# A two-layer hybrid block: the DeltaNet's chunk transitions formed ahead of the scan, attention's value products for two heads on the column halves, modulation products in pairs

## The chip, the cores and the metric

The kernel runs on one core of a Trainium2 chip. Its time is the device time of that core in microseconds (us), from runs of the same program. Everything is float32; the large products split each float32 operand into two float32r parts and take three float32r products, the small ones use float32 directly.

## What is computed

The reference runs two layers over 512 latent tokens and 256 context tokens with 1024 channels. Each layer modulates its normalised input by a shift and a scale computed from a conditioning vector, projects it once, and hands the columns to three mixers: a gated MLP over chunks of 128 tokens, attention (six query heads, two key heads of 64 channels), and a gated DeltaNet in both directions (six heads of 64). An output projection, a squared-ReLU MLP and post-norms follow. In the second layer only the latent tokens give outputs. For the change these parts matter:

```python
def _attend(q, k, v):
    s = jnp.einsum('bqhgd,bkhd->bhgqk', q, k).astype(jnp.float32) * (HEAD_DIM ** -0.5)
    pr = jax.nn.softmax(s, axis=-1).astype(v.dtype)
    return jnp.einsum('bhgqk,bkhd->bqhgd', pr, v)
...
    # gated_delta_rule, chunks of 64 tokens; u, w solve the chunk's triangular system
    def step(s, inp):
        qd, kd, u_i, w_i, a_i, gl = inp
        v_new = u_i - jnp.einsum('bhck,bhkv->bhcv', w_i, s)
        o = jnp.einsum('bhck,bhkv->bhcv', qd, s) + jnp.einsum('bhij,bhjv->bhiv', a_i, v_new)
        s = s * jnp.exp(gl)[..., None, None] + jnp.einsum('bhck,bhcv->bhkv', kd, v_new)
        return s, o
...
        mod_l = (jax.nn.silu(c) @ mod_w[i] + mod_b[i])[:, None, :]
```

## The kernel before

`Flow` interleaves streams of work, Python generators that yield after each step. Each engine runs its instructions in the order in which they were traced; `Flow.cost` guesses a duration for every instruction, and the stream whose last step ends first by that guess goes on next. Streams also wait for named signals (`conv…`, `prep…`, `made…`, `scan…`, `po…`) and for PSUM tiles, of which there are four of 512 columns ("mm") and two of 1024 ("ax").

`mix` runs one layer's mixers in three stages: input modulation with the gated MLP's projections; convolutions, query and key norms (`qk_norm`), values and the gate of z (`z_gate`), with the DeltaNet's preparation (`dn_prep`) of head pairs 0 and 1 beside them; then attention beside the scans, with `dn_prep` of pair 2. In layer 0 the last stage also holds `mods`, two pieces of the modulation (`mod`). `rest` follows with the output projection and the MLP.

In the last stage there are three scan streams, one for each pair of heads, and three streams that form their operands. The streams of the DeltaNet have a head start of 1000 ns (`BIAS`) over attention. Pairs 0 and 1 run side by side; pair 2 uses the buffers of pair 0 and its preparation must end first. A scan has six step pairs; a step pair has two steps, and each step takes one chunk forward and one backward, on the two halves of the partitions.

For each step pair `dn_make` scales keys, values and queries (gs, rU, rK), transposes some, and copies all into block-diagonal 128x128 operands in a ring of buffers (rW, rT, rK, rQ, rA), whose zero quarters GpSimd fills at the start of the stage; the triangular inverse comes in by small DMAs (rT). `dn_scan` then needs in each step, one after the other: a product with W, a subtraction (rr), a product with T, a copy (vn), a product with K and the state's update (S); where outputs are wanted, four more products and two instructions that write or add them to o. Each product runs for both heads of the pair, ten in a step. `dn_gate` norms and gates the outputs of a pair.

`attention` takes a tile of 128 queries and a head at a time: scores, maximum (amx, anm), exponential with its sum (ape), reciprocal (ars). `att_out` transposes the exponentials, copies them (apT), multiplies them by the values of both key heads (128 columns, of which 64 are used), scales the result (aot), and after six heads transposes the outputs (ayb). `mod` multiplies a conditioning vector, 32 columns wide, by 512 columns of weights at a time into one of four groups of 32 partitions of a PSUM tile.

Of the kernel before, what the change touches and what calls it, by code (L numbers as in the profile page):

```python
# [39 lines left out]
class Flow:  # L40
    """Interleaves streams of work (generators that yield after each step) as they are traced. The engines run what is
    traced in order, so the stream whose last step ends first, by a rough cost of each instruction, goes on next. A stream
    yields a generator to start it, a key to wait until that key is in `done`, a tuple of classes of PSUM tiles to get,
    or the time to go on."""

    # wait for a result of the same engine, of another one
# [68 lines left out]
    def when(self, s):  # L115
        """the time a stream can go on, None while what it waits for is not there"""
# [11 lines left out]
    def run(self, *gens, side=(), drain=False):  # L128
        """until the streams gens end; those of side go on in the next run if they have not ended, or else with drain"""
# [37 lines left out]
    def step(self, gen, val, ahead):  # L167
        """one step of a stream, its instructions as if they were traced that much earlier"""
# [19 lines left out]
    def drop(self, ap):  # L188
        """gives a PSUM tile back, after the last instruction on it"""
# [21 lines left out]
class _Core:  # L211
    """the engines, with a note of all that is issued to them"""
# [6 lines left out]
def _tb(v):  # L219
    """token tile whose chunks the backward direction takes at step pair v (the forward one takes tile v)"""  # L220
# [63 lines left out]
class K:  # L284
# [22 lines left out]
    def setup(self):  # L307
# [21 lines left out]
        nc.vector.memset(self.mhalf, -0.5)  # L329
# [1607 lines left out]
```

## Time and profile before

| | |
|---|---|
| median of 3 runs | 2101.53 us (2100.57 to 2102.2) |
| span of the profiled execution | 2099.3 us |
| TensorE busy | 1944.5 us, 93% |
| VectorE, ScalarE, GpSimd busy | 1358.6, 921.4, 195.3 us |
| stage of attention and scans, layer 0 | 304 to 576 us |
| the same, layer 1 | 1463 to 1668 us |

PE is TensorE's matmuls, PEld its weight loads, DVE is VectorE, ACT ScalarE, POOL GpSimd, SP the engine that issues the loads. The profile gives the span of one execution from its first to its last instruction; the runs' time is some 2 us longer. Busy time is the union of an engine's instructions. A float32 matmul appears as two records. Matmuls overlap in the array, so that the end of a record is not where the next may start. PEclk is the granted clock, 1.00 for 2.4 GHz and 0.50 for 1.2 GHz. What stands behind `<-` in brackets is what an idle engine waited for.

### The profile page before, as it was taken

The page shows a single profiled execution, that of the slowest core. Times are in us where ns is not written, and L with a number is a line of the kernel's source. Part 1 is how long each engine was busy: PE and PEld are TensorE (multiplying, and loading weights), DVE is VectorE, ACT ScalarE, POOL GpSimd, SP SyncE. Part 2 cuts the span into 40 slices and gives each one's busy share as a digit, 9 for nine tenths or more (in the row PEclk, how much of TensorE's full clock was granted, in tenths as well). Part 3 has the DMA queues.
Part 4 walks back from the last instruction along what each step waited for, and adds up shares of the span by engine and source line. Part 5 has one row for each costly group of instructions (what it writes and reads, how often), then busy time and mean ns, then how long its engine had stood idle before and what let it go on. Part 6 is the DMA issues. An engine that isn't in the chain of part 4 may idle for free. (4 is left out here: it accounts for less than half of the span.)

```text
span 2099.3 us, 31005 instructions
## 1 busy us (share of the span) xinstructions
PE 1944.5 (93%) x11870; PEld 1601.5 (76%) x11870; DVE 1358.6 (65%) x2659; ACT 921.4 (44%) x1881; POOL 195.3 (9%) x375
## 2 busy tenths in 40 slices
PE   6999779989898999999999989997988889999998
PEld 2887655678777888888888778875877768788886
DVE  5578887865577436362457777889896485544555
ACT  4444346566645322322232265443866445422341
POOL 1111221010012000000000111122100010000001
PEclk8999989989999999999999979977999999999999
DMA  7311024312335424241445243110101434322231
GB/s 280 103 46 51 16 75 149 117 40 64 112 110 181 132 72 159 81 140 43 139 161 173 98 142 95 53 36 26 34 23 30 166 129 164 107 90 81 96 107 59
DMA packets 98240, 208.91 MB, mean 100 GB/s; under 512 B 30850, under 2 KB 45058, under 8 KB 98092
## 3 DMA queue, kind: packets, MB, share of 16 engines
q1 hardware_dynamic: 86956, 189.24, 27.9%
q10 hardware_dynamic: 11136, 17.70, 2.2%
q8 instruction: 93, 1.52, 0.3%
q14 instruction: 55, 0.45, 0.1%
HBM read 184.38 MB, written 17.79 MB: 96 GB/s over the span
## 5 line engine op out<-in xcount | busy, mean ns | idle before, releaser
L206 ACT ACTIVATE whi<-wraw 128x1024 fp32r<-128x1024 f32 (+2 forms) x188 | 194.9, 1050 | 440.6 <-PE ax L206 287.8
L206 DVE TENSOR_TENSOR wlo<-wraw,whi 128x1024 fp32r<-128x1024 f32 (+2 forms) x188 | 226.4, 1211 | 224.6 <-ACT whi L206 224.1
L206 PE MATMUL mm<-x2xh,whi 128*128 128x256 f32 (+1 forms) x832 | 288.4, 347 | 10.5 <-ACT whi L206 9.0
L206 PE MATMUL mm<-x2xh,wlo 128*128 128x256 f32 (+1 forms) x832 | 287.3, 346 | 1.6 <-DVE wlo L206 1.6
L206 PE MATMUL mm<-x2xl,whi 128*128 128x256 f32 (+1 forms) x832 | 287.7, 346 | 0.0
L206 PE MATMUL ax<-whi,hh 128*128 128x512 f32 x640 | 251.2, 392 | 0.0
L206 PE MATMUL ax<-whi,hl 128*128 128x512 f32 x640 | 250.0, 391 | 0.0
L206 PE MATMUL ax<-wlo,hh 128*128 128x512 f32 x640 | 249.9, 390 | 0.0
L206 PEld LDWEIGHTS mm<-x2xh,whi 128*128 128x128 f32 x832 | 158.9, 191 | 34.1 <-ACT whi L206 9.4
L206 DVE TENSOR_TENSOR acc<-acc,ax 128x1024 f32<-128x1024 f32 x68 | 82.9, 1219 | 148.3 <-PE ax L206 148.1
L206 PEld LDWEIGHTS mm<-x2xh,wlo 128*128 128x128 f32 x832 | 158.6, 191 | 22.6 <-DVE wlo L206 2.4
L206 PEld LDWEIGHTS mm<-x2xl,whi 128*128 128x128 f32 x832 | 158.8, 191 | 19.9
L206 PEld LDWEIGHTS ax<-whi,hh 128*128 128x128 f32 x640 | 120.2, 188 | 29.7 <-ACT hh L206 5.2
L206 PEld LDWEIGHTS ax<-whi,hl 128*128 128x128 f32 x640 | 120.1, 188 | 27.5 <-DVE hl L206 2.9
L206 PEld LDWEIGHTS ax<-wlo,hh 128*128 128x128 f32 x640 | 120.2, 188 | 27.0 <-issue 2.6
L206 ACT ACTIVATE rl<-mm 128x256 f32<-128x256 f32 (+1 forms) x104 | 50.7, 490 | 129.1 <-PE mm L206 123.7
L206 DVE SCALAR_TENSOR_TENSOR acc<-modw,cz,acc 128x1024 f32<-128x1024 f32 x80 | 101.2, 1280 | 8.4 <-DMA acc<-in_mod_b 5.4
L206 POOL TENSOR_SCALAR rs<-mv 128x1 f32<-128x1 f32 x52 | 33.1, 637 | 699.1 <-DVE mv L206 696.8
L206 PE MATMUL mm<-ava,apT 128*128 128x128 f32 x624 | 88.4, 285 | 2.7 <-ACT apT L206 1.2
L206 PEld LDWEIGHTS mm<-ava,apT 128*128 128x128 f32 x624 | 78.8, 197 | 7.2 <-ACT apT L206 3.2
L206 DVE TENSOR_TENSOR hl<-rl,hh 128x768 fp32r<-128x768 f32 (+2 forms) x76 | 54.4, 716 | 29.4 <-ACT hh L206 29.4
L206 DVE SCALAR_TENSOR_TENSOR cacc<-cb,cw,cacc 128x772 f32<-128x772 f32 (+1 forms) x72 | 69.7, 972 | 0.7 <-ACT cacc L206 0.2
(255 smaller groups left out, 4178.5 us busy)
## 6 DMA issues: line engine op xcount, KB each, us to landing
wraw<-in_w_up SPq DMA_DIRECT2D x64, 512.0 KB
wraw<-in_w_down SPq DMA_DIRECT2D x64, 512.0 KB
modw<-in_mod_w SPq DMA_DIRECT2D x56, 512.0 KB
modw<-in_mod_w SPq DMA_DIRECT2D x80, 256.0 KB
wraw<-in_w_ch SPq DMA_DIRECT2D x22, 512.0 KB
wraw<-in_w_out SPq DMA_DIRECT2D x16, 512.0 KB
x_d<-xt ACTq DMA_DIRECT2D x16, 512.0 KB
xt<-x_d SPq DMA_DIRECT2D x14, 512.0 KB
```

The costliest lines, as they stand in the source:

```text
L206: return f(*args, **kw)
```

## The change

DeltaNet: for each step pair `dn_make` now forms, in 64x64 blocks of the two partition halves, w and u (wu), the transition of the state over a whole chunk P (the decay on the diagonal, less keys times w), its offset C, and the output's transition Q. `dn_scan` then takes P times the state plus C for each step; outputs are Q times the state plus A times u, summed over both directions once a step pair. The block-diagonal buffers, their fills, and the copies by DMA are gone. Scalings of keys and queries, the decay's diagonal and the outputs' sums move to GpSimd. A (products of queries and keys) is stored by direction, and the decays E by token. Operands of pair 2 wait for the last ones of pair 0.

Attention: 1/8 is folded into the queries, the maximum is negated as it is taken, the exponentials are divided by their sum before they are transposed, and the value products of two heads go to the two halves of the output's partitions, channels first, so that no transposition of outputs is left.

Modulation: weights come in pieces of 1024 columns, and two products on neighbouring groups are issued together. `z_gate` waits for the gate before it, the first one for all query and key norms. `Flow.cost` has new guesses for products of 64 or 32 columns of weights. In the diff below `dn_make` and `dn_scan` are shown as they are after the change, without the lines that they replace, which stand above.

```diff
+            if m == 64 and ins[0].shape[0] == 64:
+                return 0.9 * n
             if ins[-1].dtype == F32R:
                 return max(35.0 + 0.56 * m, 0.42 * n)
-            return 2.0 * max(35.0 + 0.62 * m, 0.83 * n)
+            if m == 32 and n == 512:
+                return n
+            return (1.0 if m == 64 else 2.0) * max(35.0 + 0.62 * m, 0.83 * n)
...
+        todo = [(k, g) for k in range(KD) for g in range(0, n, 2)]
...
+            nc.sync.dma_start(out=w, in_=d["mod_w"][l, j, k][:, 512 * g : 512 * g + 1024])
...
+        for i, (k, g) in enumerate(todo):
+            w = ws.pop(0)
             yield flow.ready[w.tensor.name][0]
-            nc.tensor.matmul(pm[32 * g : 32 * g + 32], self.cz[:, k, :], w, start=(k == 0), stop=(k == KD - 1))
-            if i + bufs < n * KD:
+            for b in range(2):
+                r = 32 * (g + b)
+                nc.tensor.matmul(
+                    pm[r : r + 32], self.cz[:, k, :], w[:, 512 * b : 512 * b + 512], start=(k == 0), stop=(k == KD - 1)
+                )
...
+            if p == 2:
+                yield f"made{l}05"
...
+        yield f"z{l}{t - 1}" if t > self.tiles[0] else f"qk{l}{LT[-1]}"
...
-                mx = self.small([P, 1], "amx")
-                nc.vector.tensor_reduce(out=mx, in_=ps, axis=AX.X, op=ALU.max)
                 nm = self.small([P, 1], "anm")
-                nc.vector.tensor_scalar(out=nm, in0=mx, scalar1=-0.125, scalar2=None, op0=ALU.mult)
+                nc.vector.tensor_reduce(out=nm, in_=ps, axis=AX.X, op=ALU.max, negate=True)
...
-                nc.vector.reciprocal(st["rs"][:, h : h + 1], su)
+                yield
+                rs = self.small([P, 1], "ars")
+                nc.vector.reciprocal(rs, su)
+                nc.vector.tensor_scalar(out=pe[:, 0:n], in0=pe[:, 0:n], scalar1=rs[:, 0:1], scalar2=None, op0=ALU.mult)
...
-        pT = ap_.tile([P, TOK], F32, tag="apT", bufs=1, name="apT")
+        pT = ap_.tile([P, TOK], F32, tag="apT", bufs=4, name="apT")
+        if h % 2 == 0:
+            st["pT"] = pT
...
-        po = yield from self.psum(P)
+        if h % 2 == 0:
+            self.flow.signal(f"po{l}{i}")
+            return
+        pv = yield from self.psum(P)
         for c in range(kts):
-            nc.tensor.matmul(po, pT[:, c * P : c * P + P], va[:, c].rearrange("p a b -> p (a b)"), start=(c == 0), stop=(c == kts - 1))
-        yield
-        nc.vector.tensor_scalar(out=st["ot"][:, h, :], in0=po[:, HD * (h // 3) : HD * (h // 3) + HD], scalar1=st["rs"][:, h : h + 1], scalar2=None, op0=ALU.mult)
-        self.drop(po)
+            for e, p in enumerate((st["pT"], pT)):
+                nc.tensor.matmul(
+                    pv[_half(e)], va[:, c, (h - 1 + e) // 3, :], p[:, c * P : c * P + P], start=(c == 0), stop=(c == kts - 1)
+                )
         self.flow.signal(f"po{l}{i}")
         yield
-        if h < NH - 1:
-            return
-        ot = st["ot"].rearrange("p h e -> p (h e)")
-        pt = yield from self.psum(384)
-        for a in range(3):
-            self.tr(pt[:, a * P : a * P + P], ot[:, a * P : a * P + P])
-        yield
-        y = ap_.tile([P, 3, P], F32, tag="ayb", bufs=1, name="ayb")
-        nc.scalar.copy(y, pt.rearrange("p (a b) -> p a b", a=3))
-        self.drop(pt)
-        yield from self.store(self.y_d[l, t, :, 2:5, :], y)
+        nc.scalar.copy(st["y"][:, h // 2, :], pv)
+        self.drop(pv)
+        yield
+        if h == NH - 1:
+            yield from self.store(self.y_d[l, t, :, 2:5, :], st["y"])
...
     def dn_make(self, l, p, v, qkv, G, A, TT, r):
         nc, sc = self.nc, self.dn
+        need = l == 0 or v > 1
+        kds, ks, egc, be, E = G["kds"], G["ks"], G["egc"], G["be"], G["E"]
         hs = slice(2 * p, 2 * p + 2)
+        td = (v, _tb(v))
+        a0 = 0 if l == 0 else 2
         he = lambda a: a.rearrange("p t (h e) -> p t h e", e=HD)
         q, k, vv = (he(qkv[:, w]) for w in range(3))
+        mul = lambda eng, o, a, s: eng.tensor_tensor(out=o, in0=a, in1=_col(s, HD), op=ALU.mult)
+        halves = [_half(f) for f in range(2)]
+        blk = [(d, h) for d in range(2) for h in range(2)]
+        mm = nc.tensor.matmul
+        T4 = TT.rearrange("p (d h t) c -> p d h t c", d=2, h=2)
+        new = lambda n, *sh: sc.tile([P, *sh], F32, tag=f"{n}{p % 2}", bufs=1, name=n)
+        kv, kd = new("kv", 2, 2, 2, HD), new("kd", 2, 2, HD)
+        for d, t in enumerate(td):
+            mul(nc.vector, kv[:, d, :, 0, :], k[:, t], ks[:, d, t, hs])
+        nc.scalar.copy(kv[:, 0, :, 1, :], vv[:, v])
+        mul(nc.vector, kv[:, 1, :, 1, :], vv[:, td[1]], be[:, 1, td[1], hs])
+        for d, t in enumerate(td):
+            mul(nc.gpsimd, kd[:, d], k[:, t], kds[:, d, t, hs])
+        yield
+        if need:
+            qd = new("qd", 2, 2, HD)
+            for d, t in enumerate(td):
+                mul(nc.gpsimd, qd[:, d], q[:, t], egc[:, d, t, hs])
+            yield
+        ei = new("ei", 2, 2, HD)
+        for d, t in enumerate(td):
+            nc.gpsimd.tensor_tensor(
+                out=ei[:, d], in0=self.id2.unsqueeze(1).broadcast_to([P, 2, HD]), in1=_col(E[:, d, t, hs], HD), op=ALU.mult
+            )
+        yield
+        ps = yield from self.psum(512)
+        for d, h in blk:
+            for f in halves:
+                o = P * (2 * d + h)
+                mm(ps[f, o : o + P], T4[f, d, h, td[d]], kv[f, d, h].rearrange("p a b -> p (a b)"), start=True, stop=True)
+        yield
+        wu = r["wu"]
+        nc.scalar.copy(wu.rearrange("p d h c -> p (d h c)"), ps)
+        self.drop(ps)
+        yield
+        ps, pc = yield from self.psum(512, 256)
+        for d, h in blk:
+            for i, f in enumerate(halves):
+                mm(ps[f, 256 * d + 64 * h : 256 * d + 64 * h + HD], wu[f, d, h, 0:HD], kd[f, d, h], start=True, stop=True)
+                e = i if d == 0 else 1 - i
+                o = P * e + 64 * h
+                mm(pc[halves[1 - i], o : o + HD], kd[f, d, h], wu[f, d, h, HD:P], start=True, stop=True)
+        for d, h in blk if need else ():
+            o = 256 * d + P + 64 * h
+            for f in halves:
+                mm(ps[f, o : o + HD], qd[f, d, h], self.id2[f], start=True, stop=False)
+            for f in halves:
+                mm(ps[f, o : o + HD], wu[f, d, h, 0:HD], A[f, d, h, td[d] - a0], start=False, stop=True)
+        yield
+        pv = ps.rearrange("p (d w c) -> p d w c", d=2, w=2)
+        nc.vector.tensor_tensor(out=r["P"], in0=pv[:, :, 0, :], in1=ei.rearrange("p d h c -> p d (h c)"), op=ALU.add)
+        nc.scalar.copy(r["C"].rearrange("p e c -> p (e c)"), pc)
+        if need:
+            nc.scalar.copy(r["Q"], pv[:, :, 1, :])
+        self.drop(ps, pc)
+        yield
+    def dn_scan(self, l, p, v, A, r, S, o):
         nc, sc = self.nc, self.dn
         need = l == 0 or v > 1
+        a0 = 0 if l == 0 else 2
+        td = (v, _tb(v))
         mm = nc.tensor.matmul
+        halves = [_half(f) for f in range(2)]
+        if need:
+            px, po = yield from self.psum(256, 512)
+            for d in range(2):
+                for h in range(2):
+                    for f in halves:
+                        c = P * d + 64 * h
+                        mm(po[f, c : c + HD], A[f, d, h, td[d] - a0], r["wu"][f, d, h, HD:P], start=True, stop=True)
+        else:
+            px = yield from self.psum(256)
         for e in range(2):
+            S0 = S[0]
+            w = [(h, i, f, i if e == 0 else 1 - i) for h in range(2) for i, f in enumerate(halves)]
+            for h, i, f, d in w:
+                c = P * e + 64 * h
+                mm(px[halves[1 - i], c : c + HD], r["P"][f, d, 64 * h : 64 * h + HD], S0[f, h, :], start=True, stop=True)
+            for h, i, f, d in w if need else ():
+                c = 256 + P * d + 64 * h
+                mm(po[f, c : c + HD], r["Q"][f, d, 64 * h : 64 * h + HD], S0[f, h, :], start=True, stop=True)
             yield
             S2 = sc.tile([P, 2, HD], F32, tag=f"S{p % 2}", bufs=3, name="S")
+            nc.vector.tensor_tensor(
+                out=S2.rearrange("p h c -> p (h c)"), in0=px[:, P * e : P * e + P], in1=r["C"][:, e, :], op=ALU.add
+            )
             S[0] = S2
+            yield
+        self.drop(px)
+        if not need:
+            return
+        y = po.rearrange("p (w d c) -> p w d c", w=2, d=2)
+        of = o.rearrange("p t h c -> p t (h c)")
+        yo = sc.tile([P, 2, P], F32, tag=f"yo{p % 2}", bufs=1, name="yo")
+        nc.scalar.copy(yo, y[:, 0])
+        nc.vector.tensor_tensor(out=yo, in0=yo, in1=y[:, 1], op=ALU.add)
+        self.drop(po)
+        yield
+        for d, t in enumerate(td):
+            if v == 0 or v in (2, 3):
+                nc.gpsimd.tensor_copy(of[:, t], yo[:, d])
+            else:
+                nc.gpsimd.tensor_tensor(out=of[:, t], in0=of[:, t], in1=yo[:, d], op=ALU.add)
+        yield
 
```

## Rows read from the trace of the kernel before

**Rows 1.** The page, first line.

```profile
span 2099.3 us, 31005 instructions
```

**Rows 2.** Stretches of the span in us, busy time of each engine, granted clock.

```profile
304.00:576.00 272.00, 249.06 (x2001) 193.66 (x2001) 181.16 (x602) 174.75 (x528) 25.53 (x95) 0.95 0.32 100
698.00:1211.00 513.00, 513.00 (x2585) 428.10 (x2584) 265.94 (x251) 141.16 (x182) 16.02 (x18) 1.00 0.35 116
1463.00:1668.00 205.00, 175.30 (x1672) 156.37 (x1672) 150.83 (x508) 136.70 (x405) 17.10 (x62) 0.96 0.18 54
```

**Rows 3.** Groups by shape, layer 0's stage: busy, mean ns, idle before.

```profile
L206 PE MATMUL mm<-ava,apT 128*128 128x128 f32 x336 | 47.4, 285 | 1.4 <-ACT rW L206 0.9 <-ACT apT L206 0.3
L206 PE MATMUL mm<-modw,cz 128*32 128x512 f32 x96 | 40.7, 633 | 0.0
L206 PE MATMUL mm<-S,rQ 128*128 128x128 f32 x144 | 25.2, 292 | 1.7 <-DVE aot L206 1.3 <-ACT rQ L206 0.4
L206 PE MATMUL mm<-c_ident,ape 128*128 128x128 f32 x168 | 29.6, 276 | 2.4 <-ACT ape L206 2.4
L206 DVE TENSOR_TENSOR rK<-qkv,kds 64x128 f32<-64x128 f32 x72 | 19.7, 283 | 0.8
L206 DVE TENSOR_REDUCE amx<-ax 128x1 f32<-128x768 f32 x24 | 22.8, 955 | 9.9 <-PE ax L206 9.6
```

**Rows 4.** TensorE in order of time: start us, length us, records.

```profile
319.60 1.05 PE L206 MATMUL mm<-modw,cz 128*32 128x512 f32 x4
...
398.05 0.61 PE L206 MATMUL mm<-rr,rT 128*128 128x128 f32 x4
...
548.13 0.40 PE L206 MATMUL ax<-akl,qs 128*128 128x512 f32 x1
548.36 0.28 PE L206 MATMUL ax<-akh,qs 128*128 128x256 f32 x1
```

**Rows 5.** TensorE on parts of its array; the last row has durations min/median/max.

```profile
96.75 1.62 PE L206 MATMUL mm<-gws,gv 128*64 128x128 f32 x26
...
146.00 0.68 PE L206 MATMUL ax<-kq 64*64 64x128 f32 x16
146.61 0.19 PEld L206 LDWEIGHTS mm<-xh,whi 128*128 128x128 f32 x1 [0.17 <-issue]
...
1325.31 0.47 PE L206 MATMUL ax<-kq 64*64 64x64 f32 x16
...
L206 PE MATMUL ax<-kq x32: 218/268/320, 1325.3 to 1327.7; 64*64 64x64 f32 x16, 64*64 64x128 f32 x16
```

**Rows 6.** TensorE near 431 us, and stretches of 3 us with granted clock.

```profile
431.56 1.01 PE L206 MATMUL ax<-PB,M 32*32 32x32 f32 x52 [1.76 <-DVE PB L206]
...
435.00:438.00 3.00, 3.00 (x36) 2.61 (x36) 0.66 (x4) 1.94 (x6) 0.00 (x0) 0.50 0.00 0
444.00:447.00 3.00, 3.00 (x81) 2.64 (x68) 1.84 (x8) 2.18 (x8) 1.51 (x2) 1.00 0.02 5
```

**Rows 7.** Exponentials, inverses, state updates, stores: first and last start.

```profile
L206 ACT ACTIVATE ape<-ax,anm x14: 890/901/902, 531.5 to 567.6; 128x768 f32<-128x768 f32 x14
...
L206 ACT COPY TT<-mm x8: 451/470/471, 1489.2 to 1588.3; 32x384 f32<-32x384 f32 x8
...
L206 DVE SCALAR_TENSOR_TENSOR S<-S,E,mm x24: 272/276/282, 1597.1 to 1645.1; 128x64 f32<-128x64 f32 x24
...
L206 ACTq DMA_DIRECT2D y_d<-o x6: 377/378/379, 452.6 to 1655.3; - x6
```

**Rows 8.** GpSimd's fills, and its powers in layer 0's stage.

```profile
L206 POOL MEMSET rK<- x16: 197/198/201, 1458.8 to 1470.9; 64x128 f32 x16
...
L206 POOL TENSOR_TENSOR crn<-rs,mhalf 128x12 f32<-128x12 f32 x3 | 6.9, 2316 | 0.2
```

**Rows 9.** Gates of z, and transposes of normed queries and keys.

```profile
L206 ACT ACTIVATE zth<-mm x6: 490/492/497, 280.1 to 304.0; 128x384 f32<-128x384 f32 x6
...
L206 PE MATMUL mm<-c_ident,axn x24: 271/273/329, 216.0 to 279.8; 128*128 128x128 f32 x24
```

More of the change, by code (lines that the diff above doesn't have):

```diff
@@ L329, in setup @@
         nc.vector.memset(self.mhalf, -0.5)
+        self.id2 = cp.tile([P, HD], F32, name="id2")
+        for f in range(2):
+            nc.vector.tensor_copy(self.id2[_half(f)], self.ident[_half(f), 64 * f : 64 * f + HD])
         self.cz = cp.tile([P, KD, 32], F32, name="cz")
@@ L1092, in att_out @@
         nc, ap_ = self.nc, self.a2
-        n = kts * P
         i = NH * t + h
@@ L1315, in ring @@
     def ring(self, l):
-        r = [{} for _ in range(4)]
-        for i in (0, 2, 1, 3):
-            for w, z in (("W", "W"), ("T", "A"), ("K", "K"), ("Q", "W"), ("A", "A")):
-                r[i][w] = self.bd(self.dn, z, f"r{w}{i}")
-            r[i]["U"] = self.dn.tile([P, 2, 2, HD], F32, name=f"rU{i}")
+        t = lambda n, i, *sh: self.dn.tile([P, *sh], F32, name=f"r{n}{i}")
+        r = [
+            {"wu": t("wu", i, 2, 2, P), "P": t("P", i, 2, P), "Q": t("Q", i, 2, P), "C": t("C", i, 2, P)} for i in range(4)
+        ]
         return r[:2], r[2:]
@@ L1364, in dn_prep @@
         for g in range(3):
-            need = A[g] is not None
+            a0 = 0 if l == 0 else 2
+            need = 2 * g >= a0
             nq = 2 if need else 1
@@ L1482, in dn_make @@
-        halves = [(hf, _half(hf)) for hf in range(2)]
-        def rows(w, src, sb):
-            g_ = sc.tile([P, 2, 2, HD], F32, tag=f"gs{p % 2}", name="gs")
-            mul(g_[:, :, 0, :], src[:, v], egc[:, 0, v, hs])
-            mul(g_[:, :, 1, :], src[:, b], sb[:, b, hs])
-            yield
-            ps = yield from self.psum(256)
-            for h in range(2):
-                self.tr(ps[:, 128 * h : 128 * h + P], g_[:, h].rearrange("p d e -> p (d e)"))
-            yield
-            pv = ps.rearrange("p (h e c) -> p h e c", h=2, e=2)
-            nc.scalar.copy(r[w][0:64, :, 0:4:3, :], pv[0:64])
-            for e in range(2):
-                nc.scalar.copy(r[w][64:128, :, 2 - e, :], pv[64:128, :, e, :])
-            self.drop(ps)
-            yield
@@ L1513, in dn_make @@
-        if A is not None:
-            yield from rows("Q", q, egc[:, 1])
-            for hf, f in halves:
-                nc.scalar.copy(r["A"][f, :, hf:4:2, :], A[f, v % 2])
-            yield
-    def dn_scan(self, l, p, v, G, r, S, o):
+        mul = lambda eng, o, a, s: eng.tensor_tensor(out=o, in0=a, in1=_col(s, HD), op=ALU.mult)
[3 more added lines that the diff above has]
+        T4 = TT.rearrange("p (d h t) c -> p d h t c", d=2, h=2)
@@ L1547, in dn_scan @@
             yield
             S2 = sc.tile([P, 2, HD], F32, tag=f"S{p % 2}", bufs=3, name="S")
-            for h in range(2):
-                nc.vector.scalar_tensor_tensor(
-                    out=S2[:, h, :], in0=S[0][:, h, :], scalar=E[:, v, e, 2 * p + h : 2 * p + h + 1], in1=x0[:, h],
-                    op0=ALU.mult, op1=ALU.add,
-                )
+            nc.vector.tensor_tensor(
+                out=S2.rearrange("p h c -> p (h c)"), in0=px[:, P * e : P * e + P], in1=r["C"][:, e, :], op=ALU.add
+            )
@@ L1554, in dn_scan @@
             S[0] = S2
-            self.drop(px)
             yield
-            if need:
-                po = yield from self.psum(256)
-                y = po.rearrange("p (h c) -> p h c", c=HD)[:, 0:4:3, :]
-                for w, m in (("Q", S0), ("A", vf)):
-                    for h in range(2):
-                        mm(po[:, P * h : P * h + P], c2(r[w], h), m, start=(w == "Q" and h == 0), stop=(w == "A" and h == 1))
-                yield
-                for t, hf in ((v, e), (_tb(v), 1 - e)):
-                    f = _half(hf)
-                    dst = o[f, t]
-                    if v == 0 or v in (2, 3):
-                        nc.scalar.copy(dst, y[f])
-                    else:
-                        nc.vector.tensor_tensor(out=dst, in0=dst, in1=y[f], op=ALU.add)
-                self.drop(po)
-                yield
+        self.drop(px)
```

103 lines of the change are left out of this document (21 added, 82 removed).

## The prediction

> **What bounds the kernel now.** I read the stretches first, to find where the change acts and which engine is full there. Attention and the DeltaNet scans run side by side in two stages: 272 us in layer 0, 205 us in layer 1 [rows 2]. TensorE is busy 249 and 175 us of them, at a granted clock of 0.95 and 0.96; VectorE has 181 and 151, ScalarE 175 and 137, GpSimd 26 and 17. The stretch between them is nearly all MLP, where TensorE has no gap at all [rows 2]; nothing of the change is there. So the question is what the two stages become.
>
> Busy time overstates TensorE, since a matmul's tail lies under the next one. So I next read the groups of the stage by shape [rows 3] and the spacing in the order of time [rows 4]: four records of 128x128 by 128 columns take 0.61 us, less the tail of the last (0.275, an estimate by the means of such records, 0.276 to 0.292) over three gaps is 0.112 us a record, and a float32 product is two records. A 512-column float32r product takes 0.23 us, from its start to the next, and one of 256 columns is put at half. With those prices the engine's demand in layer 0 is:
>
> - scans: ten products in each of 36 steps, five groups of 144 records like the one shown, 720 x 0.112 = 80.6
> - transposes that form their operands, 72 x 0.112 = 8.1
> - value products 336 x 0.112 = 37.6; transposes of the exponentials 168 x 0.112 = 18.8, of the head outputs 18 x 0.112 = 2.0
> - modulation products, busy 40.7 and hardly overlapping others
> - scores 24 x 0.70 + 12 x 0.24 = 19.7; some 10 for the third pair's preparation and the gates (an estimate)
>
> In all 217.5 of 272 us: 80%. Layer 1 has no modulation, and in two of six step pairs no outputs: 624 scan records 69.9, transposes 60 x 0.112 = 6.7, values 32.3, 16.1, 1.3, scores 16.8, and 10: 153 of 205 us, 75%. Where attention runs alone it takes 2.78 us a head (13 gaps from 531.5 to 567.6) [rows 7] against a demand of 0.70 + 0.67 + 1.34 = 2.71, so the engine can be filled to 97%. The rest of the stage is shared with chains that wait. TensorE is thus what bounds both stages, and a us of its demand is worth somewhat more than a us of the stage.
>
> **The change, part by part.** *Value products.* A product of 128 rows by 64 columns on each column half: 26 such records, alternating halves, took 1.62 us [rows 5], so with a tail of 0.27 they come every 0.054 us. The records stay 336 and 288: 18.1 and 15.6 us in place of 37.6 and 32.3; I add 0.17 us a pair of heads for the change between whole and part array (below), 18 and 12 times: 3 and 2. The transposes of the head outputs (2.0 and 1.3) go. The scaling by the reciprocal moves ahead of the products, onto VectorE, 768 wide; its row is missing. Bounds are the 128-column product of two tiles, 0.28, and the maximum over 768 columns, which at 22.8 us for 24 is 0.95; I take 0.6, 24 of them 14 us. What leaves VectorE in the stage of layer 0 is more: 328 instructions like the 72 key products of 0.283 (rK) [rows 3], some 92 us (keys 72, scalings gs 72, state updates 36 of 72, and rU, rr, o and head outputs 36 each). What comes: 54 such (15 us), 36 twice as wide (0.42 as an estimate, 15), the scaling (18 with the narrow tiles). So 181 becomes near 137. ScalarE, at 175, loses 252 copies and gains 102, on average twice as wide: no more than it had. Neither becomes the fuller engine.
>
> *Modulation.* Two products on neighbouring column groups, issued together, took 1.05 us for all four records [rows 4]; 48 single ones cost 40.7 [rows 3]. 24 pairs at 1.05 are 25.2: minus 15.5. Its 48 loads become 24 of twice the size; the same bytes.
>
> *DeltaNet.* A step had three dependent visits to TensorE; now the state needs one (transition times state, then one add). The rest is formed ahead, in 64x64 blocks. Sixteen records on four block positions: 0.68 us at 128 columns, 0.47 at 64 [rows 5]; less the tails (0.27 and 0.22) over fifteen gaps, 0.027 and 0.0167 a record. Much of the new code uses only two positions at a time (the diagonal ones), which I price at double: 0.053 and 0.033. One step pair with outputs: T products 16 x 0.053 = 0.85; transition and offset 32 x 0.0167 = 0.53; output transition 32 x 0.033 = 1.06; in the scan 16 x 0.033 = 0.53, and twice 16 records on four positions, pair after pair, 0.38 (between the two prices) = 0.76. That is 3.73 us. Going from blocks back to the whole array cost 0.17 us of idle in which nothing else was waited for [rows 5]; four bursts in a step pair add 0.68: 4.4 us. Before it was 20 products and four transposes, 4.9 us. Without outputs 2.6 in place of 2.9. Layer 0: 18 x 4.4 = 79 for 88.7, layer 1: 12 x 4.4 + 6 x 2.6 = 68.4 for 76.6. So the DeltaNet gives TensorE little; its other gain is the shorter chain, which leaves fewer waits to fill.
>
> The Trainium skill (TensorEngine Tiling (Array Packing), section Tiling Modes) speaks against this part: changing the tiling mode, and not only the tile, drains the engine. The 0.17 is what this trace shows of that; by a free change the DeltaNet would cost 12 us less in either layer.
>
> *Small edits.* The 144 copies by DMA of the inverses (rT) leave SP's queue. 80 fills on GpSimd of 0.2 us [rows 8], which delay the first steps of each stage, go: I leave that gain inside the share below. The gate of z waits for the query and key norms: costed at nothing, since the first z gate already starts at 280.1, after the last of their transposes at 279.8 [rows 9]; were that cover gone, a gate would come late by its own length, 0.49 us on ScalarE and two like it on VectorE. The third pair's operands wait for the first pair's last ones; the third pair's inverse comes long after them (next paragraph). The gates' 24 small products become one: nothing to minus 2 us a layer, I take nothing. The planner's new guesses can also reorder the first stages, where modulation and gated MLP have such products: nothing, with 3 us either way as an estimate.
>
> *Sum.* Layer 0: 79 + (18.1 + 3) + 18.8 + 25.2 + 19.7 + 10 = 174 us; layer 1: 68.4 + 17.6 + 16.1 + 16.8 + 10 = 129. At the same filled shares, 80% and 75%, the stages last 217 and 172: minus 55 and minus 33. What is late next is, in layer 1, the third pair: its inverse, at the end of a chain of 62 dependent instructions on VectorE, is there at 1588.3; its scan runs from 1597.1 to 1645.1, and the store behind its gate is issued at 1655.3, 10 us later [rows 7]. Even if the inverse came no sooner, scan chains with one visit for three would end it between 1588 + 19 + 10 and 1588 + 57 + 10, that is 1617 to 1655, and my stage ends at 1635. Then w_out: by the code its loads wait for buffers of this stage, and the more the streams end together, the later they start; I add 3 us, an estimate (nothing to 10). Together minus 85. The profiled span is 2099.3 us [rows 1] and the median run 2101.5, 2.2 more; I subtract from the median: 2016 us.
>
> **Rivals.**
> *The clock.* After 1.76 us without work at 429.8, TensorE's granted clock fell; from 435 to 438 it was 0.50 (1.2 GHz) with the engine busy 3.00 of 3 us in small blocks mixed with whole products, and it was at 2.4 GHz again only in the stretch from 444 [rows 6]. After the change more of the work is small blocks and bursts with gaps. If the granted mean falls from 0.95 to c, the stages grow to 217 x 0.95 / c and 172 x 0.96 / c: at 0.85 they are 437 us in all, minus 40 (2064 with w_out's 3). Below c = 0.78, more than two fifths of the time at 1.2 GHz, the kernel is slower; at 0.72, 516 us, plus 39: 2144. For it: that stretch. Against it: from 1500 to the end of the scans the engine was no fuller than I forecast, and the clock of the whole stage was 0.96 [rows 2]. Slower by this: 0.07; a gain cut to below 45 us: 0.12.
> The Trainium skill (TensorE: Matmul & The Clock Gate, Part 1) has the half clock as the default, which activity releases; the rows of 431 to 447 agree.
>
> *Blocks don't overlap.* If two diagonal positions ran one after the other, step pairs cost another 2.4 us (0.85 + 1.06 + 0.53), 43 us in layer 0 and 34 in layer 1: at the same shares the stages last 271 and 217, plus 11, and w_out's 3: 2116. Against it: sixteen records in 0.68 us can only come from positions that run at once. 0.03.
>
> *GpSimd as the bound.* Eight instructions in a step pair (four without outputs) move to it: 144 and 120. Nearest rows: a 64x128 fill takes 0.2 us, a power of 12 columns 2.3 [rows 8]; ordinary products are nearer the fill; I take 0.8, 115 and 96 us, hidden. It bounds layer 0 from 1.5 us each; at 1.7 the stages would be 245 and 204, minus 28: 2077 with w_out. 0.05.
> The Trainium skill (GPSIMD Engine Reference, section 3) makes a two-input product about twice as slow there as on VectorE, which from 0.283 us is 0.57 (an estimate); no run here shows it.
>
> *Fuller.* Shorter chains and idle VectorE and ScalarE could lift the filled share to 90% in layer 0 (193) and, bounded by the third pair's end, 150 us in layer 1: minus 134, 1970 with w_out. 0.15.
>
> **How the numbers follow.** The forecast has 0.55 (1988 to 2050, shares within six points of before); fuller 0.15; a cut gain (clock) 0.12; GpSimd 0.05; slower by clock or blocks 0.10; within 0.2%, about 4 us, which is what a measurement of this kernel can tell from no change, 0.03. Faster thus 0.87. The range reaches from the fuller case, 1962, to the cut gains, 2080.
>
> **What would show it.** Value products as 128x64 records 0.05 us apart; 24 modulation pairs of 1.05 us; 64x64 bursts of 0.5 to 1.1 us, some 0.17 of idle behind them; the layer 0 stage near 217 and layer 1's near 172 us; granted clock at 0.93 or more; GpSimd under 130 us in layer 0; third pair's scan under 40 us. The prediction is wrong if the clock falls below 0.85 in these stages, if TensorE's share stays under 70% with no engine full (then PSUM tiles, of which a scan now holds two for a whole step pair, or GpSimd's latency bind), or if the time moves outside the two stages.

## The result and the profile after

The change takes 2041.11 us (median of 4 runs, 2039.17 to 2043.16) where the kernel before took 2101.28 beside it: a ratio of 0.9717, interval 0.9703 to 0.9731. It is faster by 60 us; I had said 85, with 2016 us inside 1962 to 2080.

The page's first line of the kernel after answers to [rows 1]: 61.9 us shorter.

```profile
span 2037.4 us, 35195 instructions
```

The stretches answer to [rows 2], in the same columns (layer 0's stage, the same length of MLP, layer 1's stage):

```profile
309.00:537.00 228.00, 194.38 (x3303) 141.59 (x3302) 146.94 (x354) 130.32 (x367) 74.02 (x158) 0.93 0.33 107
684.00:1197.00 513.00, 509.61 (x2583) 428.33 (x2582) 280.05 (x276) 147.60 (x201) 20.92 (x29) 0.99 0.37 118
1424.00:1608.00 184.00, 148.90 (x2890) 120.89 (x2882) 124.92 (x301) 111.69 (x291) 60.93 (x132) 0.91 0.15 47
```

To compare kernels I cut each trace at the same four events: the first fill of the state S on GpSimd, and the end of the instruction that issues a stage's last store to y_d, in either layer. Before, that gives 304.9 us up to layer 0's stage, 269.8 in it, 882.2 between, 211.3 in layer 1's stage, 431.0 behind. After: 309.1, 228.2, 886.6, 184.5, 429.0. So the gain is 41.6 + 26.8 inside the stages, where I had 55 + 33, and 8.6 us are lost ahead of them, less 2.0 behind. No engine is full: TensorE's busy share fell from 92% to 85% and from 86% to 81%, and the others' shares are below 70%.

The groups by shape in layer 0's stage answer to [rows 3]:

```profile
L213 PE MATMUL mm<-apT,ava 128*64 128x128 f32 x336 | 29.0, 284 | 4.9 <-ACT apT L213 4.3 <-DVE yo L213 0.5
L213 PE MATMUL mm<-modw,cz 128*32 128x512 f32 x96 | 28.6, 641 | 2.2 <-DVE yo L213 2.2
...
L213 POOL TENSOR_TENSOR kd<-qkv,kds 128x128 f32<-128x128 f32 x36 | 17.4, 502 | 35.0 <-PE mm L213 35.0
...
L213 DVE TENSOR_SCALAR ape<-ape,ars 128x768 f32<-128x768 f32 x24 | 15.0, 625 | 1.0
```

TensorE in order of time, against [rows 4, 5]: value products on column halves, a modulation pair, and blocks of an output transition.

```profile
331.04 1.05 PE L213 MATMUL mm<-modw,cz 128*32 128x512 f32 x4
...
448.01 0.32 PE L213 MATMUL mm<-id,qd 64*64 64x64 f32 x4
448.12 0.32 PE L213 MATMUL mm<-A,rwu 64*64 64x64 f32 x4
...
448.82 0.32 PE L213 MATMUL mm<-A,rwu 64*64 64x64 f32 x4
449.07 0.44 PE L213 MATMUL mm<-c_ident,ape 128*128 128x128 f32 x2
...
503.63 1.52 PE L213 MATMUL mm<-apT,ava 128*64 128x128 f32 x22
```

And the landmarks of [rows 7] (count, durations min/median/max, first and last start): the last inverse of layer 1, the third pair's state updates behind it, the stores of both layers, and the exponentials left over behind the scans in layer 0.

```profile
L213 ACT COPY TT<-mm x8: 468/470/473, 1452.3 to 1549.9; 32x384 f32<-32x384 f32 x8
...
L213 DVE TENSOR_TENSOR S<-mm,rC x12: 283/291/292, 1557.4 to 1587.1; 128x128 f32<-128x128 f32 x12
...
L213 ACTq DMA_DIRECT2D y_d<-ayb x10: 326/330/339, 411.0 to 1608.0; - x10
L213 ACTq DMA_DIRECT2D y_d<-o x6: 377/378/412, 401.7 to 1599.9; - x6
...
L213 ACT ACTIVATE ape<-ax,anm x17: 893/907/944, 486.7 to 531.6; 128x768 f32<-128x768 f32 x17
```

The third pair's scan took 48 us in layer 1 and takes 30. What ends both stages is the attention (y_d<-ayb), as it was before, and the last 17 heads of layer 0 follow one another at (531.6 - 486.7) / 16 = 2.81 us, where it was 2.78 [rows 7], though their value products now take less than half as long.

### The profile page after: what moved, and what is told of

Same layout as the page of the kernel before. It is cut to its first block, busy times and chain, and to the rows that moved or that the text cites. A ratio compares the mean times of both kernels' runs of the same rounds, so it can differ in the third digit from the quotient of the medians.

```text
span 2037.4 us, 35195 instructions
## 1 busy us (share of the span) xinstructions
PE 1859.2 (91%) x14496; PEld 1519.5 (75%) x14496; DVE 1284.2 (63%) x2165; ACT 854.5 (42%) x1607; POOL 279.2 (14%) x479
## 4 chain that ended last, share of the span: by engine, by line
PE 61%; DVE 18%; issue 7%; ACT 5%; POOL 4%; DMA 3%; SPq 0%; ACTq 0%; POOLq 0%; DVEq 0%
PE mm L213 37%; PE ax L213 25%; DVE cacc L213 2%; DVE Xx L213 2%; DVE tm L213 2%; DVE wlo L213 2%; POOL crn L213 2%; DVE M L213 1%; DMA wraw<-in_w_up 1%; POOL rs L213 1%; DVE anm L213 1%; ACT ape L213 1%; DVE st L213 1%; POOL arn L213 1%; ACT osq L213 1%
## 5 line engine op out<-in xcount | busy, mean ns | idle before, releaser
L213 POOL MEMSET acc<- 128x1024 f32 x10 | 9.5, 955 | 468.9 <-PE mm L213 468.9
L213 DVE TENSOR_REDUCE anm<-ax 128x1 f32<-128x768 f32 (+1 forms) x60 | 50.6, 848 | 33.3 <-PE ax L213 33.2
```

Of the source, the lines that this page charges most:

```text
L213: return f(*args, **kw)
```

## The experiments

Each kernel ran beside the kernel before on its chip. The stages are cut as above. The medians of the kernel before were between 2098.6 and 2102.0 us on these chips, so a difference of a few us between rows is read from the ratios and not from the times.

```
kernel                  us       ratio [95%]               ahead  stage 0  between  stage 1  behind
the change              2041.11  0.9717 [0.9703, 0.9731]   309.1  228.2    886.6    184.5    429.0
dn_only                 2047.27  0.9756 [0.9736, 0.9775]   304.9  227.7    891.0    186.0    433.6
no_attention            2053.41  0.9780 [0.9759, 0.9800]   308.6  229.1    890.3    184.3    434.4
no_mod_pairs            2029.36  0.9663 [0.9647, 0.9679]   303.9  222.3    886.4    186.5    428.7
hold_psum               2061.98  0.9820 [0.9801, 0.9838]   311.9  234.3    886.1    199.5    429.1
pairs_old_price         2036.67  0.9687 [0.9673, 0.9701]   304.7  229.0    886.4    186.3    429.2
no_division             2032.10  0.9672 [0.9647, 0.9697]   308.6  221.6    885.8    177.9    432.7
inverse_cut             2029.83  0.9659 [0.9643, 0.9675]   311.9  225.7    887.0    172.7    429.4
attention_first         2023.81  0.9628 [0.9614, 0.9643]   312.0  216.8    887.1    186.9    420.2
single_first            2033.19  0.9690 [0.9674, 0.9706]   304.0  226.5    891.6    188.8    419.5
single_first_l0         2034.60  0.9696 [0.9681, 0.9710]   302.4  222.8    889.0    186.8    428.5
single_first_split_po   2035.10  0.9695 [0.9680, 0.9710]   306.9  229.1    890.4    189.9    419.5
single_first_vector     2024.11  0.9643 [0.9628, 0.9657]   302.8  223.1    888.4    188.0    421.1
```

**The DeltaNet alone, and the change without the attention's part.** The first takes attention, modulation and the planner's price for the modulation's products from the kernel before; the second only the attention:

```diff
-                rs = self.small([P, 1], "ars")
-                nc.vector.reciprocal(rs, su)
-                nc.vector.tensor_scalar(out=pe[:, 0:n], in0=pe[:, 0:n], scalar1=rs[:, 0:1], scalar2=None, op0=ALU.mult)
...
-                nc.tensor.matmul(
-                    pv[_half(e)], va[:, c, (h - 1 + e) // 3, :], p[:, c * P : c * P + P], start=(c == 0), stop=(c == kts - 1)
-                )
+            nc.tensor.matmul(po, pT[:, c * P : c * P + P], va[:, c].rearrange("p a b -> p (a b)"), start=(c == 0), stop=(c == kts - 1))
```

> Only the DeltaNet part of the change is made; attention's value products and the modulation products stay as before. Theory of demand (TensorE's work sets the stages): the DeltaNet takes only 9.7 us of demand away in layer 0 and 8.2 in layer 1, so about 20 to 25 us of the 60 come from it. Theory of chains (the length of the scan's dependent steps sets the stages, TensorE is no longer full): the DeltaNet alone brings 45 us or more.

> The change without its attention part (value products over 128 columns, scaling and transposes behind them as before). Demand: attention took 18.5 and 18.0 us from TensorE, so 40 us of the gain are missing, about 2080 us. Chains: attention alone still took 2.8 us a head in the last 50 us of layer 0's stage, as before, so little is missing: under 12 us, about 2045 to 2053 us.

The DeltaNet alone brings 53 of the 60 us. In the stages it brings all of it: 227.7 and 186.0 against the full change's 228.2 and 184.5. With the attention's part left out they are 229.1 and 184.3, so in the stages that part is worth 0.9 and -0.2 us. The 12 us between the two medians are 9.4 in the profiled runs, and those lie in the stretches that follow the stages: 3.7 between and 5.4 behind; why, no run shows. Beside single modulation products the attention's part is worth more: the kernel without pairs (below) differs from the DeltaNet alone by this part only, and has 222.3 and 186.5 us against 227.7 and 186.0 in the stages, and 18 us less in all.

That the DeltaNet's part gives the gain is shown; through what is not. By my prices it takes 9.7 and 8.2 us of TensorE's work away, at the shares before 23 us of the stages, and the stages lost 42.1 and 25.3. So most of it is not TensorE's work. The same edit shortens the scan's chain, takes fills and DMA copies out, and relieves VectorE and ScalarE (181 and 175 us busy in layer 0's stage before, 141 and 131 by the next row, of the DeltaNet alone); no run parts these.

```profile
305.00:533.00 228.00, 208.26 (x3320) 159.28 (x3320) 140.63 (x384) 131.03 (x355) 74.41 (x158) 0.99 0.33 107
```

What the attention's part did to the last heads of layer 0, where no DeltaNet work is left, shows in a windows row of 44 us, for the DeltaNet alone:

```profile
486.00:530.00 44.00, 43.69 (x340) 40.07 (x339) 25.02 (x63) 30.97 (x68) 0.00 (x0) 1.00 0.21 75
```

and for the change:

```profile
487.00:531.00 44.00, 38.76 (x318) 30.60 (x318) 28.45 (x52) 31.17 (x74) 0.00 (x0) 0.96 0.46 155
```

With the old products TensorE is full (43.69 of 44) and a head takes, by the next row, (525.5 - 488.1) / 13 = 2.88 us:

```profile
L210 ACT ACTIVATE ape<-ax,anm x14: 900/902/904, 488.1 to 525.5; 128x768 f32<-128x768 f32 x14
```

With the new ones TensorE has 5 us of gaps, no other engine is full, and a head takes as long. The work left TensorE and the time stayed.

**Without the division.** What came into the head's chain is the scaling by the reciprocal. This run leaves it out:

```diff
-                nc.vector.tensor_scalar(out=pe[:, 0:n], in0=pe[:, 0:n], scalar1=rs[:, 0:1], scalar2=None, op0=ALU.mult)
```

> The change with the scaling of the exponentials by the reciprocal of their sum left out (the attention's outputs are not divided by the softmax sum): 0.61 us and one hand-over to VectorE and back less between a head's exponential and its transposes. Theory 'attention's own chain': with the value products cheap, a head goes on at 2.8 us because its steps follow one another (maximum 0.96, exponential 0.91 and its sum 0.21, reciprocal 0.16, scaling 0.61, transposes 0.88, copies), while TensorE is at 37.8 of 44 us in the last heads of layer 0 (40.7 of 44 in the kernel before). Then heads come at 2.2 to 2.5 us and the kernel is 8 to 20 us faster than the change: 2021 to 2033 us. Rival 'TensorE or its PSUM tiles': the period stays at 2.7 to 2.8 us and the time within 4 us of 2041.

Its heads, once the third pair's gate is through:

```profile
L213 ACT ACTIVATE ape<-ax,anm x16: 892/904/908, 491.3 to 525.4; 128x768 f32<-128x768 f32 x16
```

They come at (525.4 - 491.3) / 15 = 2.27 us, 0.5 us less than the change's 2.81, for an instruction of 0.62 us on an engine that was busy 28 of 44. Both stages are 6.6 us shorter, the median 9. So the scaling stands in the chain that sets the head's period, and in these heads the attention's own chain is what the TensorE gain turned into. Without it TensorE is busy 34.16 of 36 us again, near its limit:

```profile
491.00:527.00 36.00, 34.16 (x320) 29.05 (x320) 19.24 (x37) 31.21 (x75) 0.00 (x0) 1.00 0.45 153
```

**The third inverse cut short.**

```diff
-        for j in range(31):
+        for j in range(31 if p < 2 else 7):
```

> The change with the loop of the third pair's triangular inverse cut from 31 to 7 steps (the rest of that inverse is left out): its chain of 62 VectorE instructions, 39 us long in both kernels, becomes some 9 us. Theory 'third pair's chain': it holds the third scan and so the end of each stage; the time falls by 20 to 30 us in each layer, to 1980 to 2000 us. Rival 'attention comes last': the third scan starts earlier, but the heads left over at the end go on at 2.8 us each, and only what VectorE and the order gain shows: 2025 to 2040 us in all. In between, near 2010 us, both hold, one in layer 0 and the other in layer 1.

```profile
L213 ACTq DMA_DIRECT2D y_d<-ayb x10: 326/326/338, 422.8 to 1597.0; - x10
L213 ACTq DMA_DIRECT2D y_d<-o x6: 377/378/380, 405.9 to 1576.0; - x6
```

Its state updates in layer 0 and in layer 1:

```profile
L213 DVE TENSOR_TENSOR S<-mm,rC x36: 274/292/292, 329.0 to 461.4; 128x128 f32<-128x128 f32 x36
...
L213 DVE TENSOR_TENSOR S<-mm,rC x36: 273/283/292, 1435.1 to 1564.2; 128x128 f32<-128x128 f32 x36
```

and in the change, layer 0:

```profile
L213 DVE TENSOR_TENSOR S<-mm,rC x36: 277/291/293, 326.6 to 470.8; 128x128 f32<-128x128 f32 x36
```

11 us in all, inside the rival's range: layer 0's stage gives 2.5 us and layer 1's 11.8, though by the last starts of S the third scan ends, from the stage's start, 12 us sooner in layer 0 (461.4 - 311.9 against 470.8 - 309.1) and 23.5 in layer 1 (1564.2 - 1424.5 against 1587.1 - 1423.9). In layer 0 the chain is covered by the heads that are left; in layer 1 half of it shows. Also with the cut, the attention stores last.

**Attention in front.**

```diff
-        flow.run(*chains, self.attention(l, at), [prep(2), BIAS], ...
+        flow.run(*chains, [self.attention(l, at), BIAS], [prep(2), BIAS], ...
```

> The change with the attention given the same head start in the order's plan as the DeltaNet's streams have (1000 ns), so that fewer heads are left when the third scan ends. Theory 'attention comes last' (17 heads follow the third scan in layer 0, at 2.8 us, with TensorE not full): 5 to 20 us faster than the change, 2021 to 2036 us. Rival 'DeltaNet's chain sets the end': its instructions now stand behind the attention's on each engine, the third inverse comes later by some 10 us in each layer, and the time is 2045 to 2065 us.

This is the fastest kernel of the study, 0.9628 [0.9614, 0.9643], 17 us better than the change, as the first theory had it.

```profile
L213 ACTq DMA_DIRECT2D y_d<-ayb x10: 326/327/333, 377.4 to 1560.9; - x10
L213 ACTq DMA_DIRECT2D y_d<-o x6: 377/377/379, 398.6 to 1602.5; - x6
```

Layer 0's stage falls from 228.2 to 216.8, the length I had forecast for the change, while its third scan ends 30 us later (last start of S at 501.1, against 470.8): attention had been the late one. In layer 1 the attention now ends 42 us ahead of the DeltaNet; the stage gains nothing (186.9), but the stretch behind it is 9 us shorter.

**The modulation: no pairs, and pairs under the old price.** The first takes the modulation's products singly, as before, and removes the planner's price; the second keeps the pairs and removes the price only:

```diff
-            if m == 32 and n == 512:
-                return n
```

> The change without the modulation in pairs (pieces of 512 columns, products issued one by one). Demand: 15.5 us of TensorE in layer 0 come back, 18 us slower than the change, about 2059 us. Chains: these products lie in the first 100 us of the stage, where TensorE has the most work beside them; between 5 and 18 us slower.

> The change with the modulation products in pairs and their 512 KB loads, but with the order's planner pricing a product of 32 rows and 512 columns as the kernel before did (850 ns instead of 512). Leaving out pairs and price together measured 2029.4 us (ratio 0.9663), 12 us better than the change. If the price did the harm (it moves the order that the planner writes, already in the stretch before layer 0's stage, which starts at 303.9 instead of 309.1 us), this one measures about 2029 us, a ratio of 0.965 to 0.968. If the pairs themselves or their larger loads did it, it stays near the change: 2037 to 2045 us, 0.970 to 0.974.

Both theories of the first were wrong: without the pairs the kernel is 12 us faster than the change. The price alone is worth 4 of that, all of it ahead of layer 0's stage (309.1 to 304.7; 303.9 without pairs, 304.9 in the kernel before). Leaving out the pairs as well gives the other 7, in layer 0's stage: 229.0 against 222.3 (the intervals of the two ratios just overlap). Beside the old attention pairs and price cost little there: 229.1 without the attention's part, 227.7 with the DeltaNet alone. The rows of the change and of the kernel without pairs:

```profile
L213 PE MATMUL mm<-modw,cz x96: 592/617/1061, 331.0 to 414.6; 128*32 128x512 f32 x96
L213 SPq DMA_DIRECT2D modw<-in_mod_w x24: 327/328/585, 309.5 to 404.5; - x24
```

```profile
L210 PE MATMUL mm<-modw,cz x96: 592/604/617, 320.5 to 449.0; 128*32 128x512 f32 x96
L210 SPq DMA_DIRECT2D modw<-in_mod_w x48: 327/328/1075, 304.5 to 438.2; - x48
```

In pairs the 96 records are through in 84 us, singly they spread over 129. 122 us into its stage the change has begun 11 exponentials and the kernel without pairs 14. That fits an attention that is late and that the modulation pushes back further, but no run moved the modulation alone, so it is argued, not shown.

The granted clock is a second explanation, which no run here tests. From 414 to 434 us the modulation is through in the change and goes on in the kernel without pairs:

```profile
414.00:434.00 20.00, 17.21 (x254) 12.03 (x251) 10.22 (x22) 15.06 (x46) 2.57 (x3) 0.66 0.14 41
```

```profile
414.00:434.00 20.00, 18.95 (x308) 10.73 (x310) 9.26 (x19) 12.32 (x39) 5.89 (x10) 1.00 0.52 163
```

Over layer 0's stage the clock is 0.93 with pairs and the old price and 0.98 without pairs, so some 32 and 9 us of it were at 1.2 GHz. These 23 us more could cost up to 12 (an estimate, for an engine that is full in them), and so all of the 7. Against it: with the attention in front and the pairs kept, the clock was 0.94 and the stage 216.8 us.

**A PSUM tile less.** A stream of its own holds one of the four tiles of 512 columns through each stage.

```diff
+        def hold():
+            ps = yield from self.psum(512)
+            yield f"o{l}2"
+            self.drop(ps)
+            yield
```

> The change, with one of the four 512-column PSUM tiles taken away for the whole stage of attention and scans, in both layers; no work is added or left out. If PSUM tiles hold the streams up (a scan holds two for a whole step pair, two scans run at once, the modulation keeps one), the stages grow by more than 40 us together. If they don't, by under 10 us.

It costs 21 us, 6.1 in layer 0's stage and 15.0 in layer 1's, between my two figures (over 40, under 10). By the waits of layer 1's stage (engine, line, waited for: us, times, longest), with a tile less:

```profile
POOL kd L213 <- PE mm L213: 57.1, 12, 31.8
...
ACT rwu L213 <- PE mm L213: 24.1, 15, 6.8
DVE anm L213 <- PE ax L213: 17.6, 13, 7.4
DVE kv L213 <- PE mm L213: 14.1, 8, 6.5
```

and in the change:

```profile
POOL kd L213 <- PE mm L213: 51.9, 8, 34.6
...
DVE anm L213 <- PE ax L213: 15.0, 12, 7.4
ACT rwu L213 <- PE mm L213: 14.4, 13, 2.8
...
DVE kv L213 <- PE mm L213: 3.9, 4, 2.4
```

So the tiles matter, most in layer 1; one less is felt by the DeltaNet's steps (rwu and kv, 10 us of waiting more each).

**Combinations.** They start from the kernel without pairs and with the attention in front (single_first); then the head start in layer 0 only; one PSUM tile at a time in a scan step, its output products behind it; and kd and qd on VectorE:

```diff
-                mul(nc.gpsimd, qd[:, d], q[:, t], egc[:, d, t, hs])
+                mul(nc.vector, qd[:, d], q[:, t], egc[:, d, t, hs])
...
-            px, po = yield from self.psum(256, 512)
+        px = yield from self.psum(256)
...
+            yield self.dn_outs(l, p, v, A, r, used, o)
```

> The change without the pairs of modulation products and without their new price, and with the attention's head start of 1000 ns: the two edits that measured 2029.4 and 2023.8 us by themselves. If both help because the attention is what ends last in layer 0, they overlap there, and what adds is the 5 us that the order ahead of that stage gains: 2016 to 2022 us (0.960 to 0.962). If they were separate gains they add: 2010 to 2014 us (0.956 to 0.958).

> As single_first, but the attention has its head start in layer 0's stage alone. With the head start in both layers the attention's last store in layer 1's stage stood at 1560.9 us and the third pair's last state at 1592.9, so there the DeltaNet ends last. If the head start costs in layer 1 (attention in front of the third preparation), this one is 2 to 8 us faster than single_first; if the layer 1 gained from it as well, it is 3 to 8 us slower.

> As single_first, but each scan step takes one PSUM tile while its two state steps run, and the products that make its output are issued after them in a stream of their own with a tile that is taken only then (the state tiles have five buffers for that, the modulation's pieces come three ahead). Taking one of the four tiles away cost 21 us. If tiles held through the scan steps' waits keep the other streams off TensorE, this is 5 to 15 us faster than single_first; if the tiles are free often enough, it is within 4 us of it.

> As single_first, but the scaled keys and queries of the preparations (kd, qd) are formed on VectorE instead of GpSimd, which the first preparation of the stage waits 8.5 us for. If GpSimd's two-input operations hold the chain, this is 4 to 12 us faster than single_first; if they are off the path (GpSimd is busy in 74 of layer 0's 228 us and 61 of layer 1's 184) and VectorE's added work counts instead, it is the same to 5 us slower.

The two best edits don't add: together 0.9690, worse than the attention in front alone (0.9628) and no better than the single products alone (0.9663). Layer 0's stage goes back to 226.5 with a start at 304.0, while the pairs with the attention in front had 216.8. So my expectation for the sum failed in both its forms: the same head start takes 11.4 us off layer 0's stage beside the pairs (228.2 to 216.8) and adds 4.2 beside single products (222.3 to 226.5). What it is worth depends on the rest of the order, which each edit reshuffles. The head start in layer 0 alone is the same within the intervals, which neither of my two figures had, 3.7 us shorter there, 2.0 in layer 1 and 9 longer behind it. Splitting the scan's tiles gave nothing, as if the tiles were free often enough there. GpSimd's products on VectorE gave 9 us by the medians and 7.1 by the profiled runs, of which 4.2 lie in the stages and the rest around them; with the order free to move that is a hint that GpSimd's latency stands in the chain, not a proof.

## Why the prediction was right, and where its working failed

- *The place held, the mechanism only in part, and the sum came near in part by luck.* The gain lies in the two stages, as forecast. But by my prices and shares 23 of their 88 us were the DeltaNet's and 65 the attention's and the modulation's. Measured, the stages lost 67 us with the DeltaNet alone, and 1 more with the other two. The first is nearly three times its forecast, the second nearly nothing, and the two errors cancel in large part.
- *The third pair came out as forecast.* The third pair's scan came to 34 us in layer 0 and 30 in layer 1 (forecast under 40), and its gate's store ended at 1600.3.
- *The prices held.* Value products: 22 records in 1.52 us, less a tail of 0.27 over 21 gaps 0.060 (0.054 forecast). The output transition's 32 records began in eight groups, 0.116 us apart from 448.01 to 448.82: 0.029 a record (0.033 forecast). GpSimd's operations took 0.50 us, not 0.8, and its busy time in layer 0 was 74 us (115 forecast, 130 the limit), so as a full engine that rival is out; its latency, by the run with kd and qd on VectorE, is not. VectorE came to 147 us (137 forecast; its list adds up to 324 instructions, not 328, which is 92 us either way). The modulation came to 28.6 us, not 25.2. The kernel before already had some products overlapped with a neighbour (x4 records in [rows 4]), so pairs were no new thing there.
- *The step that failed is "at the same filled shares".* Cut at the events used here, my demand filled 217.5 of 269.8 us (81%) and 153 of 211.3 (72%) before; after it is 174 of 228.2 (76%) and 129 of 184.5 (70%). In the gain that is 13 and 6 of the missing 25 us; of the rest, 3.6 are that 6.6 us were lost outside the stages, where I had 3. I had taken the DeltaNet's part as little demand and shorter chains, and the other two as TensorE time that the stage gives back. With the DeltaNet alone the shares rose, to 91% and 78% (207.8 of 227.7 us and 144.8 of 186.0), in layer 0 as in my rival "fuller"; with the other two they fell again, since TensorE's time in attention gave 0.9 and -0.2 us in the stages beside the pairs, and 5.4 and -0.5 beside single products. My 2.71 us of TensorE in a head's 2.78 was nearly right for the kernel before (busy 34.29 of 36 us from 531). I had costed the scaling at 0.6 us and it took 0.62, but on VectorE's account, where there is room, and not on the head's chain, where it is worth 0.5 us a head.
- *"Minus 15.5" for the modulation had the wrong sign:* beside the new attention the pairs cost 7 us in the stage, and the new price 4 ahead of it; why is open, as said above. I had "3 us either way" for the planner's guesses.
- *Costed at nothing, z's wait on the query and key norms:* in layer 0 nothing indeed, since the DeltaNet alone, which has that wait, starts its stage at 304.9 like the kernel before. The 4.4 us between the stages aren't settled: in layer 1 the first gate of z starts at 1411.3, 0.7 us behind the last such transpose, so there the wait may bind.
- *The clock is not settled.* It was 0.93 and 0.91 in the stages, less than before and in layer 1 less than my limit. By the formula of my rival that is 222 and 181 us in place of 217 and 172, 14 of the 20 us that are missing there. The runs don't bear out so high a price: the kernel without pairs had 0.87 from 1413 to 1599, where the formula asks 8 us more than the change's, and was 2 us longer; and the DeltaNet alone had 0.99 from 305 to 533, a stage of the same length. But these kernels differ in more than their clock.
- *The third pair's chain* is the wait that is late next in layer 1, as forecast, for 12 us of 30 that a cut takes from it; in layer 0 it is covered.
- *Open:* which order of the streams is best, and how much of any single edit here is its own effect and how much the planner's new order. With the attention in front, layer 0's stage was 216.8 us with the modulation in pairs and 226.5 without.

## What to carry to other kernels

An engine at 80 or 90% of a stretch is not a demand that can be sold back at the same share: first ask what the work it loses turns into, and whether the operation that comes in its place stands in the chain of the stream that ends last. Here 0.7 us a head left TensorE (12 records of 0.112 and then 12 of 0.054 to 0.060) and 0.6 us a head came into the chain, and the period stayed at 2.8 us. And where a planner writes the order, try its head starts: one number there was worth 17 us, but nothing beside another edit, so gains of that kind don't add.

## What the runs showed of the hardware

- The change from 64x64 blocks back to whole products stands by itself once: the last group of a burst starts at 448.82, the next whole product at 449.07, 0.25 us later with no wait shown, where groups follow each other at 0.116. That is some 0.13 us for the change (0.17 priced). Over a stage its cost isn't shown. I had priced 12 us a layer; the waits for nothing shown, at the loading of weights in layer 0's stage, rose by 4 in all, from these before:

```profile
PEld mm L206 <- issue: 15.0, 30, 1.7
...
PEld ax L206 <- issue: 4.9, 8, 0.8
```

  to these in the change:

```profile
PEld mm L213 <- issue: 18.4, 46, 1.6
...
PEld ax L213 <- issue: 5.4, 19, 0.8
```

  What else it cost would lie under other waits. The Trainium skill (TensorEngine Tiling (Array Packing), section Tiling Modes) says that a change of mode drains the engine; no run here contradicts that.
- A product of two 128x128 inputs on GpSimd took 0.50 us and on VectorE 0.35 (the row of kd above, 502 ns, against this one). The Trainium skill (GPSIMD Engine Reference, section 3) has a factor of about two for such operations; by these rows it is 1.4 at this size.

```profile
L213 DVE TENSOR_TENSOR kv<-qkv,ks 128x128 f32<-128x128 f32 x36 | 11.3, 348 | 4.0 <-PE mm L213 3.9
```
